# Early transposed chunks and row copies issued from the scalar engine's queue, and the gates and first splits of the second expert product placed ahead of the last chunks

## The chip, the cores and the metric

The kernel runs on one core of one Trainium2 chip. A core has TensorE (PE; its weight loads are shown as PEld), VectorE (DVE), ScalarE (ACT), GpSimd (POOL) and SyncE (SP), each with an instruction queue of its own that runs in order; transfers are issued from the queues of SP, ACT or POOL and carried out by 16 DMA engines. The metric is the device time of one execution in microseconds, the median of several runs; lower is better.

## The reference

One hybrid decoder layer in float32: 256 tokens, model width 1024.

```python
h = rmsnorm(x, mix_norm_g)
rq, rk, rv, rg, mq, mk, mv, ga, gb = split(h @ w_in)            # w_in: 1024 x 6656
ret = retention(rotary(rq), rotary(rk) / 8, rv)                  # 8 heads, chunks of 128, group norm
y_a = (ret * silu(rg)) @ ret_w_branch
att = moba_attention(norm(mq), norm(mk), mv, rel_bias)           # one block of 256: causal softmax with a bias
y_b = att @ moba_w_branch
x = x + (sigmoid(ga) * y_a + sigmoid(gb) * y_b) @ w_out
h2 = rmsnorm(x, ffn_norm_g)
# PEER: 8 heads, 128 x 128 = 16384 experts, the best 16 of each head
q = (h2 @ peer_w_q).reshape(T, 8, 2, 128)
s = einsum('thcd,hcnd->thcn', q, sub_keys)
experts, gates = top16 of the 16 x 16 sums of the two top16, softmax
a = gelu(einsum('td,thkd->thk', h2, u_tab[experts]))
x = x + einsum('thk,thkd->td', gates * a, v_tab[experts])
```

## The kernel before, in words

The order of the instructions on each engine is written by hand: Python loops emit them, and every engine works through its own in that order. There are three stages.

*Mixer and queries* (pieces). Every weight matrix is cut into pieces of 256 rows by 512 columns; `pieces` holds 72 for the mixer (`n_mixer`) and 16 for the PEER queries. In iteration i, `load_to(i + 1)` issues loads into `raw_ring` (six tiles of 512 KB) on SP; `cut(i + 3)` splits a landed piece into a high and a low part (ACT writes `rhi`, L136; DVE writes `rlo`, L137); `products(i)` runs three products of PE for each pair (L217 to L219 or L226 to L228); `pump` advances up to three generators with the epilogues of the units, attention (L348, L354, L366, L367), rotary (L310, L259), retention, and `residual` (L513, L517, transposes L526).

*Early chunks.* The tables `peer_u` and `peer_v` are walked in 128 chunks of 128 experts. The first product of the PEER part needs a chunk of `peer_u` transposed. For one chunk in eight (`STEP`), NPRE = 16 in all, that is done in the mixer stage by `early_turns(i)`: four reads of 128 KB bring a chunk in blocks (L672), two stream transposes on DVE turn it (L677, half a chunk each), and a write stores it in the DRAM tensor `turned` (L674). The buffers `early[0]` (`eraw`, and `h`, the tile `h2`) and `early[1]` (`eT`, and `hTf`) alternate. The reads and writes are issued from SP's queue.

*First expert product* (chunks c = 0 to 127). `transpose_u(c + 2)` turns a chunk by eight transposes of PE into the `turn` banks (L661; four banks, two for each chunk) and two copies of ACT (L662), or, for an early chunk, takes what `load_any` read from `turned`. Then 16 products of PE (L1114) give 144 of the 192 dense tokens their scores; `product_evac` puts a Gelu on them, two chunks at a time (L1075, L1078), POOL multiplies with the gates (L1076). Beside it run

- `gather(GATHER)`, 0.95 steps a chunk: `fetch` gathers rows of `peer_u`, later of `peer_v`, by index on POOL (L911) for the tokens that are not dense; `dot_v` (L922) and the running sum `vacc` (L983 on ACT for the first row, L985 on DVE) take them up;
- `chain_step(BUDGET)`: generators that yield their cost, of which 1.28 are spent a chunk: eight `topk` (t = 0, 1 and q = 0 to 3), then `dense_gates`. This one works on groups of four tokens: `one_hots` builds two sets of one-hots on DVE (L1012, L1013), ACT scales four of them by the gates (L1015), PE multiplies them (L1048) two steps later (`LAG_G`), and `gates_evac` writes the result into `W` (L1059 on DVE, L1061 on ACT). A step costs `GSTEP` = 1.25.

Ahead of the chunks, 24 small copies (L1097) bring rows of `h2x` from DRAM into three tiles `h2r`, issued from SP. At the end of the stage the PSUM pools are closed, `cut_v` splits V chunks (L136, L137), and `cut_w` splits two chunks of the gates `W` into `cw` (L1090 on ACT, L1091 on DVE).

*Second expert product.* For each chunk, eight `block`s of two products (L1140, L1141) accumulate in all eight PSUM banks; `gather(GATHER_V)` takes half a step a chunk. In chunk 125 the copies for the last sums are issued; then DVE adds the gathered sum (L1166, L1167), and `add_up` (L1173, L1174) and `turn_back` (L1179 to L1182) bring the banks back and add them to the residual.

Of the kernel before, what the change touches and what calls it, by code (L numbers as in the profile page):

```python
# [20 lines left out]
P = 128  # L21
# [22 lines left out]
LAG_G = 2  # L44
SCRATCH = 88
TOPK = 16
NPRE = 16
STEP = 128 // NPRE
PRE0 = 4
SK = 16  # L50
NP = H * TOPK
NJ = NP // 2
# [11 lines left out]
def layer_kernel(ctx, tc, x, mix_norm_g, w_in, ret_w_branch, moba_q_gain, moba_k_gain, moba_w_branch,  # L64
# [37 lines left out]
    def lo_tile(dt=F32R):  # L102
        return rg.tile([P, 1024], dt, name="rlo_", tag="rlo", bufs=4)
# [21 lines left out]
    def pump(n=3):  # L125
        for g in list(tasks)[:n]:
            if g in tasks:
                advance(g)
# [494 lines left out]
    def load_any(i):  # L623

        if sk_at <= i < sk_at + 2:
            r = raw_tile().rearrange("p (j i) -> p j i", j=H)
            nc.sync.dma_start(r, peer_sub_keys[0].rearrange("h c n d -> n (h c) d")[:, H * (i - sk_at):H * (i - sk_at + 1), :])
            sk_raw.append(r)
            return
        i -= 2 * (i >= sk_at)  # L630
        if i < len(pieces):
            load(i)
        elif i < len(pieces) + NK:
            c = i - len(pieces)
            if c % STEP == STEP - 1:
                u_raw[c] = raw_tile()
                nc.sync.dma_start(u_raw[c], turned[c // STEP])
            else:
                u_raw[c] = load_rows(peer_u, c)
        elif i < len(pieces) + 2 * NK:  # L640
            v_raw[i - len(pieces) - NK] = load_rows(peer_v, i - len(pieces) - NK)
# [8 lines left out]

    def transpose_u(c):

        if c < NK and c % STEP == STEP - 1:
            u_T[c] = u_raw.pop(c)
        elif c < NK:
            r = u_raw.pop(c)
            u_T[c] = hi_tile(F32)
            for q in range(2):
                p = psum["turn"].tile([P, 512], F32, name="turn")
                for k in range(4):  # L660
                    T.transpose(p[:, k * P:(k + 1) * P], r.rearrange("p (i k) -> p k i", k=KC)[:, 4 * q + k], ident)  # L661
                A.activation(u_T[c][:, 512 * q:512 * (q + 1)], p, AF.Copy)  # L662

    def early_turns(i):

        m, step = divmod(i - PRE0, 4)
        if step == 0 and -1 <= m < NPRE - 1:

            c = STEP * (m + 1) + STEP - 1
            src = peer_u[0, c * P:(c + 1) * P, :].rearrange("(b a) (g d) -> g a b d", a=32, g=4)  # L670
            for g in range(4):
                nc.sync.dma_start(early[0][(m + 1) % 2][32 * g:32 * g + 32].rearrange("a (b d) -> a b d", b=4), src[g])  # L672
        if step == 1 and 0 < m <= NPRE:
            nc.sync.dma_start(turned[m - 1], early[1][(m - 1) % 2])  # L674
        if step % 2 == 0 and 0 <= m < NPRE:
            k = slice(2 * step, 2 * step + 4)
            V.transpose(early[1][m % 2].rearrange("p (k b a) -> p b k a", k=KC, b=4)[:, :, k],  # L677
                        early[0][m % 2].rearrange("p (b i k) -> p b k i", b=4, k=KC)[:, :, k])

# [65 lines left out]
    for i in range(n_mixer + 3):  # L745
        load_to(i + 1)
        cut(i + 3)
        products(i)
        pump()
        early_turns(i)  # L750
    while tasks:
        pump()
    dump("x1", xt)
# [55 lines left out]
    def topk(t, q, s_sb):  # L809
# [60 lines left out]
        if q < 3:  # L870
            return
        g = gates[:, t].rearrange("p (h k) -> p h k", h=H)
        A.activation(g, g, AF.Exp)
        yield 2.0
        sm = tk.tile([P, H], F32, name="sm")
# [131 lines left out]
    def one_hots(oh_buf, t, k, slot):  # L1007

        buf, slot = (oh_buf, slot) if slot < 8 else (oh_more, slot - 8)
        o2, o1 = buf[:, 0, slot:slot + 4], buf[:, 1, slot:slot + 4]  # L1010
        i1, i2 = (tT[:, t, j, k:k + 4, None].to_broadcast([P, 4, NK]) for j in range(2))
        V.tensor_tensor(o2, niota[:, None, :].to_broadcast([P, 4, NK]), i2, op=OP.is_equal)  # L1012
        V.tensor_tensor(o1, iota[:, None, :].to_broadcast([P, 4, NK]), i1, op=OP.is_equal)  # L1013
        for j in range(4):
            A.activation(o1[:, j], o1[:, j], AF.Copy, scale=tT[:, t, 2, k + j:k + j + 1])  # L1015
        return [(o2[:, j], o1[:, j]) for j in range(4)]

    full = []

    def gates_finish():  # L1020
        while full:
            gates_evac(*full.pop())

    def dense_gates():

        def columns(t):
            p = psum["turn"].tile([P, 512], F32, name="turn")
            for j, src in enumerate((i12f[:, t, 0], i12f[:, t, 1], gates[:, t])):
                T.transpose(p[:, j * P:(j + 1) * P], src, ident)
            A.activation(tT[:, t, :3], p[:, :3 * P].rearrange("p (j i) -> p j i", j=3), AF.Copy)  # L1030

        yield 2.0
        columns(1)
        yield 0.1
        V.tensor_scalar(niota, iota, -1.0, None, op0=OP.mult)
        oh_buf = cp.tile([P, 2, 8, NK], F32, name="oh_buf", tag="b8")
        built = []
        for n0 in range(0, ND + 4 * LAG_G, 4):
            gates_finish()
            if n0 == P - 8:  # L1040
                while not gs["xdone"]:
                    gather_step()
                columns(0)
            if len(built) == LAG_G or (n0 >= ND and built):
                n1, oh = built.pop(0)
                p = psum["gates"].tile([P, 512], F32, name="gp")
                for j, (o2, o1) in enumerate(oh):
                    T.matmul(p[:, j * P:(j + 1) * P], o2, o1, start=True, stop=True)  # L1048
                full.append((n1, p.rearrange("p (t i) -> p t i", t=4)))
            if n0 < ND:  # L1050
                t, k0 = (1, n0) if n0 < P else (0, n0 - P + NG)
                built.append((n0, one_hots(oh_buf, t, k0, n0 % 12)))
            yield GSTEP
# [37 lines left out]
            V.tensor_tensor(w[:, :, ND:], W[:, c:c + 2, :], w[:, :, :ND].bitcast(F32), op=OP.subtract)  # L1091
            w_cut[c] = w

    h2r = [lo_tile(F32) for _ in range(NXG)]
    for n in range(NXG):
        for h in range(H):
            nc.sync.dma_start(h2r[n][NXP * h:NXP * (h + 1)], h2x[NXP * n:NXP * (n + 1)])  # L1097
    for c in range(TAHEAD):
        transpose_u(c)
    for c in range(NK):  # L1100
        load_to(len(pieces) + c + TAHEAD)
        gates_finish()
        transpose_u(c + TAHEAD)
        if c and c % 2 == 0:
# [9 lines left out]
            T.matmul(pa[:, n:n + NA], uT[:, k * P:(k + 1) * P], hTf[:, k], start=(c % 2 == 0 and k == 0),  # L1114
                     stop=(k == KC - 1), skip_group_check=True)
        pump()
        gather(GATHER)
        chain_step(BUDGET)
        if c >= NK - 2:
            load_to(len(pieces) + c + 3)  # L1120
            cut_v(c - (NK - 2))
    while chain:
        chain_step(9.0)
        gates_finish()
    product_evac(NK - 2, pa)


    cps.close()
    psum["acc"] = ctx.enter_context(tc.tile_pool(name="psv", bufs=KC, space=bass.MemoryType.PSUM))
    cw = cp.tile([P, 2, D], F32R, name="cw", tag="b8")[:, :, :4 * ND].rearrange("p s (c t) -> p s c t", c=2)  # L1130

    o = [acc() for _ in range(KC)]
    cut_w(0)
    half = P - NG
    res, late = {}, []

# [112 lines left out]
```

## Time and profile before

| | us |
|---|---|
| median of 3 runs | 1028.72 (1023.83 to 1029.67) |
| profiled execution, its time | 1027.87 |
| profiled execution, its span | 1026.1 |
| PE busy in it | 999.1 |
| DVE busy | 812.5 |
| ACT busy | 549.0 |
| POOL busy | 305.3 |

The span runs from the first to the last instruction of the profiled execution; the execution's own time has what lies around it too. Times in the rows of the profile are microseconds from the span's start, unless they are marked as nanoseconds. A line such as L1114 is a line of the kernel before. In a row of waits the engine before the arrow stood idle until the instruction behind it ended. In a row of the timeline the first number is the start and the second the duration; PE's rows are pipelined, so that their durations overlap.

### The profile page before, as it was taken

Reading aid. Unit: us, or ns where it says so; the run is one execution under the profiler, and the core shown is the slowest. Engines: PE = TensorE matmul, PEld = TensorE weight load, DVE = VectorE, ACT = ScalarE, POOL = GpSimd, SP = SyncE. Lnnn points to the kernel's source line nnn. Section 1 sums busy time; section 2 is a strip of 40 time slices with the busy share of each in tenths; the row PEclk is TensorE's granted clock in tenths of the full one; section 3 lists DMA queues with packets and bytes.
Section 4 is the critical chain, followed back from the end, with each engine's and each line's share of the span. In section 5 each row is a group of like instructions: output and inputs, shape, how many; then the busy total and the mean of one; then the engine's idle time right before and its main releaser. Section 6 shows DMA issues by size and latency. Waiting matters only on the chain.

```text
span 1026.1 us, 19479 instructions
## 1 busy us (share of the span) xinstructions
PE 999.1 (97%) x7364; PEld 963.7 (94%) x7364; DVE 812.5 (79%) x1483; ACT 549.0 (54%) x989; POOL 305.3 (30%) x258
## 2 busy tenths in 40 slices
PE   6989999999999999999999999999899999999998
PEld 5877998997998999999999999999899999999997
DVE  5767566879589894699978798973888888888886
ACT  5534554534553435443467687686455555555553
POOL 2411010000103443444343333544433333333310
PEclk9999999999999999999999999999999999999999
DMA  9876665797657997999997767787999999999983
GB/s 319 244 222 195 224 220 172 259 303 240 210 196 245 400 370 283 343 371 383 391 387 264 289 241 263 294 309 280 334 338 346 340 351 336 352 336 355 334 300 111
DMA packets 104123, 301.44 MB, mean 294 GB/s; under 512 B 11052, under 2 KB 21829, under 8 KB 103901
## 3 DMA queue, kind: packets, MB, share of 16 engines
q1 hardware_dynamic: 77164, 204.95, 57.0%
q0 software_dynamic: 26864, 95.25, 25.7%
q8 instruction: 58, 0.95, 0.4%
q14 instruction: 37, 0.30, 0.1%
HBM read 288.62 MB, written 10.95 MB: 292 GB/s over the span
## 4 chain that ended last, share of the span: by engine, by line
PE 87%; DMA 5%; issue 2%; DVE 2%; ACT 2%; POOL 1%; SPq 0%; DVEq 0%; POOLq 0%; ACTq 0%
PE acc L1114 21%; PE acc L1140 20%; PE acc L1141 9%; PE turn L661 8%; PE acc L217 4%; PE acc L226 4%; PE acc L227 3%; PE acc L228 3%; PE acc L218 3%; PE acc L219 3%; PE gp L1048 3%; DMA raw_ring<-in_w_out_dram 2%; PE side L568 1%; POOL rows L911 1%; DMA rows<-in_peer_u_dram,eg 1%
## 5 line engine op out<-in xcount | busy, mean ns | idle before, releaser
L911 POOL DMA_INDIRECT rows<-in_peer_u_dram,eg x112 | 131.8, 1177 | 123.0 <-DVE rows L922 47.2
L911 POOL DMA_INDIRECT rows<-in_peer_v_dram,eg x64 | 103.4, 1616 | 165.4 <-DVE vacc L985 163.8
L661 PE MATMUL turn<-ident,raw_ring 128*128 128x128 f32 x896 | 117.6, 274 | 2.2 <-DMA raw_ring<-in_peer_u_dram 1.3
L661 PEld LDWEIGHTS turn<-ident,raw_ring 128*128 128x128 f32 x896 | 109.0, 191 | 2.8 <-issue 1.8
L922 DVE SCALAR_TENSOR_TENSOR rows<-rows,h 128x1024 f32<-128x1024 f32 x64 | 78.4, 1229 | 18.8 <-DMA rows<-in_peer_u_dram,eg 17.6
L985 DVE SCALAR_TENSOR_TENSOR vacc<-rows,av,vacc 128x1024 f32<-128x1024 f32 x63 | 80.5, 1278 | 14.6 <-ACT vacc L983 12.9
L1090 ACT ACTIVATE cw<-W 128x384 fp32r<-128x384 f32 x64 | 33.7, 527 | 82.6 <-PE acc L1141 36.4
L1091 DVE TENSOR_TENSOR cw<-W,cw 128x384 fp32r<-128x384 f32 x64 | 36.3, 567 | 36.3 <-ACT cw L1090 36.3
L1015 ACT ACTIVATE oh_buf<-oh_buf,tT 128x128 f32<-128x128 f32 x128 | 41.2, 394 | 26.8 <-DVE oh_buf L1013 25.8
L1076 POOL TENSOR_TENSOR W<-W,gl 128x288 f32<-128x288 f32 (+17 forms) x27 | 24.1, 892 | 92.5 <-ACT gl L1075 80.2
L1059 DVE TENSOR_TENSOR W<-gp,W 128x360 f32<-128x360 f32 (+17 forms) x36 | 35.4, 983 | 8.5 <-PE gp L1048 7.2
L1114 PE MATMUL acc<-hTf,raw_ring 128*128 128x144 f32 x256 | 34.0, 286 | 0.0
L1048 PE MATMUL gp<-oh_buf 128*128 128x128 f32 x256 | 33.7, 275 | 0.0
L1114 PEld LDWEIGHTS acc<-hTf,raw_ring 128*128 128x128 f32 x256 | 32.3, 190 | 0.0
L1048 PEld LDWEIGHTS gp<-oh_buf 128*128 128x128 f32 x256 | 31.4, 192 | 0.0
L1061 ACT ACTIVATE W<-gp 128x512 f32<-128x512 f32 (+18 forms) x48 | 28.0, 584 | 6.1 <-DVE W L1059 2.3
L531 POOL DMA_DIRECT2D x1d<-xt x1 | 0.7, 652 | 92.0 <-DVE xt L513 92.0
L922 DVE SCALAR_TENSOR_TENSOR rows<-rows,rlo__3153 128x1024 f32<-128x1024 f32 x16 | 19.4, 1215 | 10.2 <-DMA rows<-in_peer_u_dram,eg 10.2
L143 POOL TENSOR_TENSOR gny<-va,minus_half 128x8 f32<-128x8 f32 x2 | 4.4, 2182 | 76.9 <-DVE va L433 76.9
L1015 ACT ACTIVATE oh_more<-oh_more,tT 128x128 f32<-128x128 f32 x64 | 20.6, 396 | 11.1 <-DVE oh_more L1013 11.1
L1012 DVE TENSOR_TENSOR oh_buf<-niota,tT 128x512 f32<-128x512 f32 x32 | 23.1, 722 | 2.8 <-ACT tT L1030 2.8
L1013 DVE TENSOR_TENSOR oh_buf<-iota,tT 128x512 f32<-128x512 f32 x32 | 22.0, 689 | 0.0
(2082 smaller groups left out, 3476.5 us busy)
## 6 DMA issues: line engine op xcount, KB each, us to landing
raw_ring<-in_peer_v_dram SPq DMA_DIRECT2D x128, 512.0 KB
raw_ring<-in_peer_u_dram SPq DMA_DIRECT2D x112, 512.0 KB
raw_ring<-in_w_in_dram SPq DMA_DIRECT2D x52, 512.0 KB
raw_ring<-in_peer_w_q_dram SPq DMA_DIRECT2D x16, 512.0 KB
raw_ring<-turned SPq DMA_DIRECT2D x16, 512.0 KB
eraw<-in_peer_u_dram SPq DMA_DIRECT2D x32, 128.0 KB
h<-in_peer_u_dram SPq DMA_DIRECT2D x32, 128.0 KB
turned<-eT SPq DMA_DIRECT2D x8, 512.0 KB
```

Source lines behind the costliest of these rows:

```text
L217: T.matmul(o[t], xh[:, s], wh, start=(k == 0), stop=False)
L226: T.matmul(d, wh[:, s], xh, start=(k == 0 and b % 2 == 0), stop=False, skip_group_check=True)
L661: T.transpose(p[:, k * P:(k + 1) * P], r.rearrange("p (i k) -> p k i", k=KC)[:, 4 * q + k], ident)
L911: G.indirect_dma_start(out=r, out_offset=None, in_=tab, in_offset=bass.IndirectOffsetOnAxis(ap=eg[:, j:j + 1], axis=0))
L922: V.scalar_tensor_tensor(r, r, 1.0, h, op0=OP.mult, op1=OP.mult, accum_out=av[:, j:j + 1])
L985: V.scalar_tensor_tensor(gs["acc"], r, av[:, j:j + 1], gs["acc"], op0=OP.mult, op1=OP.add)
L1015: A.activation(o1[:, j], o1[:, j], AF.Copy, scale=tT[:, t, 2, k + j:k + j + 1])
L1048: T.matmul(p[:, j * P:(j + 1) * P], o2, o1, start=True, stop=True)
L1091: V.tensor_tensor(w[:, :, ND:], W[:, c:c + 2, :], w[:, :, :ND].bitcast(F32), op=OP.subtract)
L1114: T.matmul(pa[:, n:n + NA], uT[:, k * P:(k + 1) * P], hTf[:, k], start=(c % 2 == 0 and k == 0), stop=(k == KC - 1), skip_group_check=True)
L1140: T.matmul(o[b][:, :2 * ND], vh[:, n], w, start=(c == 0), stop=False, skip_group_check=True)
L1141: T.matmul(o[b][:, :ND], vl[:, n], w[:, :ND], start=False, stop=(c == NK - 1), skip_group_check=True)
```

## The change

- NPRE is 15, STEP stays 8, and PRE0 is 5: chunk 127 is turned by PE with the others. The reads and the write of an early chunk are issued from ACT's queue, the write at step 3 of the same chunk instead of step 1 of the next; the two transposes stand in neighbouring iterations (steps 0 and 1, not 0 and 2), and `early_turns` runs ahead of `pump`.
- The row copies for `h2r` are issued from ACT's queue, eight in each of the first three chunks.
- In `topk` a `yield 3.0` stands ahead of the Exp. In `dense_gates` the scaling of one-hots on ACT (`factors`) is issued one step after the one-hots, behind PE's products of the step.
- At the end of the first product the gather stops in the last three chunks. In chunk 124 the rest of the chain is issued at once and `cw` is allocated; `cut_v(0)`, `cut_w(0)` and `cut_v(1)` follow in chunks 125, 126 and 127.

```diff
-NPRE = 16
-STEP = 128 // NPRE
-PRE0 = 4
+NPRE = 15
+STEP = 8
+PRE0 = 5
...
-            if c % STEP == STEP - 1:
+            if c % STEP == STEP - 1 and c // STEP < NPRE:
...
             for g in range(4):
-                nc.sync.dma_start(early[0][(m + 1) % 2][32 * g:32 * g + 32].rearrange("a (b d) -> a b d", b=4), src[g])
-        if step == 1 and 0 < m <= NPRE:
-            nc.sync.dma_start(turned[m - 1], early[1][(m - 1) % 2])
-        if step % 2 == 0 and 0 <= m < NPRE:
-            k = slice(2 * step, 2 * step + 4)
+                nc.scalar.dma_start(early[0][(m + 1) % 2][32 * g:32 * g + 32].rearrange("a (b d) -> a b d", b=4), src[g])
+        if step == 3 and 0 <= m < NPRE:
+            nc.scalar.dma_start(turned[m], early[1][m % 2])
+        if step < 2 and 0 <= m < NPRE:
+            k = slice(4 * step, 4 * step + 4)
...
         products(i)
+        early_turns(i)
         pump()
-        early_turns(i)
...
         g = gates[:, t].rearrange("p (h k) -> p h k", h=H)
+        yield 3.0
         A.activation(g, g, AF.Exp)
...
-        for j in range(4):
-            A.activation(o1[:, j], o1[:, j], AF.Copy, scale=tT[:, t, 2, k + j:k + j + 1])
-        return [(o2[:, j], o1[:, j]) for j in range(4)]
+        def factors():
+            for j in range(4):
+                A.activation(o1[:, j], o1[:, j], AF.Copy, scale=tT[:, t, 2, k + j:k + j + 1])
+        return [(o2[:, j], o1[:, j]) for j in range(4)], factors
...
+            if built:
+                built[-1][1][1]()
             if n0 < ND:
...
-    h2r = [lo_tile(F32) for _ in range(NXG)]
-    for n in range(NXG):
-        for h in range(H):
-            nc.sync.dma_start(h2r[n][NXP * h:NXP * (h + 1)], h2x[NXP * n:NXP * (n + 1)])
+    h2r = []
+    def rows_x(n):
+        if n < NXG:
+            h2r.append(lo_tile(F32))
+            for h in range(H):
+                nc.scalar.dma_start(h2r[n][NXP * h:NXP * (h + 1)], h2x[NXP * n:NXP * (n + 1)])
...
         load_to(len(pieces) + c + TAHEAD)
+        rows_x(c)
         gates_finish()
...
-        gather(GATHER)
+        if c < NK - 3:
+            gather(GATHER)
         chain_step(BUDGET)
-        if c >= NK - 2:
+        if c == NK - 4:
+            while chain:
+                chain_step(9.0)
+                gates_finish()
+            cw = cp.tile([P, 2, D], F32R, name="cw", tag="b8")[:, :, :4 * ND].rearrange("p s (c t) -> p s c t", c=2)
+        if c >= NK - 3:
             load_to(len(pieces) + c + 3)
-            cut_v(c - (NK - 2))
-    while chain:
-        chain_step(9.0)
-        gates_finish()
+        if c == NK - 3:
+            cut_v(0)
+        elif c == NK - 2:
+            cut_w(0)
+        elif c == NK - 1:
+            cut_v(1)
     product_evac(NK - 2, pa)
...
-    cw = cp.tile([P, 2, D], F32R, name="cw", tag="b8")[:, :, :4 * ND].rearrange("p s (c t) -> p s c t", c=2)
     o = [acc() for _ in range(KC)]
-    cut_w(0)
```

More of the change, by code (lines that the diff above doesn't have):

```diff
@@ L651, in transpose_u @@
     def transpose_u(c):
-        if c < NK and c % STEP == STEP - 1:
+        if c < NK and c % STEP == STEP - 1 and c // STEP < NPRE:
             u_T[c] = u_raw.pop(c)
@@ L1046, in dense_gates @@
                 p = psum["gates"].tile([P, 512], F32, name="gp")
-                for j, (o2, o1) in enumerate(oh):
+                for j, (o2, o1) in enumerate(oh[0]):
                     T.matmul(p[:, j * P:(j + 1) * P], o2, o1, start=True, stop=True)
                 full.append((n1, p.rearrange("p (t i) -> p t i", t=4)))
+            if built:
+                built[-1][1][1]()
             if n0 < ND:
```

## The prediction

> **What bounds the kernel.** I read the page's busy times first, then the waits of TensorE (PE), then what ended each of them. On the page:
>
> ```profile
> span 1026.1 us, 19479 instructions
> PE 999.1 (97%) x7364; PEld 963.7 (94%) x7364; DVE 812.5 (79%) x1483; ACT 549.0 (54%) x989; POOL 305.3 (30%) x258
> PE 87%; DMA 5%; issue 2%; DVE 2%; ACT 2%; POOL 1%; SPq 0%; DVEq 0%; POOLq 0%; ACTq 0%
> ```
>
> TensorE is busy for 97% of the span and is 87% of the chain that ended last. A change can win only where PE waits (27 us in all), or by leaving PE work out; whatever lies on another engine costs nothing until PE waits for it. The waits of TensorE (us in total, times, longest):
>
> ```profile
> PE acc L1140 <- DVE cw L1091: 4.0, 1, 4.0
> PE side L259 <- POOL ra L310: 1.8, 1, 1.8
> PE side L526 <- DVE xg L517: 1.8, 1, 1.8
> PE gp L1048 <- ACT W L1061: 1.4, 1, 1.4
> PE turn L661 <- DMA raw_ring<-in_peer_u_dram: 1.3, 1, 1.3
> PE side L366 <- ACT pr L354: 1.0, 1, 1.0
> PE acc L218 <- DVE rlo__2252 L137: 0.3, 1, 0.3
> ```
>
> The first is the passage from the first expert product (L1114) to the second (L1140). The windows over it (columns: window, length, busy PE, PEld, DVE, ACT, POOL, granted clock, DMA share, GB/s) show a second loss behind it:
>
> ```profile
> 719.00:723.00 4.00, 0.03 (x1) 0.01 (x1) 3.61 (x4) 3.13 (x5) 3.53 (x4) 1.00 0.76 252
> 724.30:727.80 3.50, 3.50 (x16) 3.50 (x15) 2.88 (x4) 1.06 (x1) 1.69 (x1) 0.51 1.02 417
> ```
>
> PE stands for 4.0 us, and then runs 3.5 us at a granted clock of 0.51: 3.5 x 0.49 = 1.7 us more. The passage costs 5.7 us.
>
> **The change part by part.** *The passage.* Today the splits of the first V chunks and of the gates (`cut_v`, `cut_w(0)`) stand after the last U chunks, and DVE has sums of gathered rows (L985) between them (a product of one chunk from the chain of waits, then the timelines of ACT and DVE):
>
> ```profile
> 606.84 1.96 PE acc L1114 x16
> 715.52 1.05 ACT L136 ACTIVATE rhi__7415<-raw_ring 128x1024 fp32r<-128x1024 f32 x1
> 719.13 0.41 ACT L1075 ACTIVATE gl<-acc 128x288 f32<-128x288 f32 x1 [1.62 <-PE acc L1114]
> 719.44 0.52 ACT L1090 ACTIVATE cw<-W 128x384 fp32r<-128x384 f32 x1
> 719.39 1.28 DVE L985 SCALAR_TENSOR_TENSOR vacc<-rows,av,vacc 128x1024 f32<-128x1024 f32 x1 [0.82 <-DMA rows<-in_peer_v_dram,eg]
> 720.60 1.22 DVE L137 TENSOR_TENSOR rlo__7432<-raw_ring,rhi__7431 128x1024 fp32r<-128x1024 f32 x1
> 721.73 1.15 DVE L1091 TENSOR_TENSOR cw<-W,cw 128x384 fp32r<-128x384 f32 x1
> ```
>
> After the change `cut_v(0)`, `cut_w(0)` and `cut_v(1)` are issued in chunks 125 to 127, with no gather between, while PE still has two to three products of 1.96 us to do. ACT's share in that time is one Gelu (0.41), the gates (0.52) and two splits of 1.05. So only the last Gelu (L1075) stands between the products: 0.4 us. Gain 4.0 + 1.7 - 0.4 = 5.3 (at most 5.7, at least 3 should a PSUM bank or DVE be late).
>
> *The drained gates.* This is the price. Each of the two `topk` tails (t = 0 and 1) gets a `yield 3.0`, together 6.0 of a budget of 1.28 a chunk: the dense gates end 4.7 chunks later. Their last step stands in chunk 121 now; it would be 125 to 126, but all is drained at chunk 124 (NK - 4). Counting the credit step by step, the group products (L1048) popped at n0 = 180 and 184 fall in chunks 122 and 123, and three (188, 192, 196) in chunk 124. In that chunk each group needs its four factors (L1015), which now stand one step ahead of it, behind ACT's other work. From the chain of waits around 690 us and the timelines of PE, ACT:
>
> ```profile
> 608.80 0.89 PE gp L1048 x8
> 609.69 0.89 PE turn L661 x8
> 694.25 0.95 ACT W L1061
> 695.20 0.91 ACT rhi__7205 L662 x2
> 696.11 1.17 ACT oh_more L1015 x4
> 712.11 1.16 ACT L983 ACTIVATE vacc<-rows,av 128x1024 f32<-128x1024 f32 x1
> ```
>
> From the start of chunk 124, ACT (with 0.2 us of latency) takes the last group (0.95), the turned chunk (0.91), a Gelu (0.41), the first gathered V row (1.1), factors (1.17): 4.8; then a group (0.95) and factors (1.17): 6.9. PE's own work before its third group product is 0.89 + 1.96 + 2 x 0.89 = 4.6. PE waits 6.9 - 4.6 = 2.3 us. Without the V row in that place it would be 1.2; with ACT 1.7 late, 4.0. I take 2.3.
>
> *Chunk 127 is turned on PE* (NPRE 15): eight transposes more, the row of 0.89. Cost 0.9, not hidden.
>
> *The last early turn goes away*, and the queue is changed. DVE's timeline just before the residual:
>
> ```profile
> 244.12 1.20 DVE L677 STREAM_TRANSPOSE hTf<-h 128x512 f32<-128x512 f32 x1
> 247.49 1.14 DVE L677 STREAM_TRANSPOSE hTf<-h 128x512 f32<-128x512 f32 x1
> 248.56 1.17 DVE L137 TENSOR_TENSOR rlo__2308<-raw_ring,rhi__2307 128x1024 fp32r<-128x1024 f32 x1
> ```
>
> DVE is late there and PE waits for it: 0.3 (L218) and 1.8 (L526), 2.1 us. The two transposes shown belong to the 16th early chunk and are gone: 2.3 us less on DVE. I book the 2.1 as gained. Below nothing: the other 15 are done in neighbouring pieces and ahead of `pump`, so an epilogue may wait 1.1 us more on DVE; bounds 0 to 2.3.
>
> *Early reads and writes on ACT's queue.* On SP they block what is behind them, the loads of weights (first two rows: the DMA queue's own waits; then durations min/median/max of the issues in ns; the last row is ACT's load in the windows):
>
> ```profile
> SPq L672 <- DVE eT L677: 65.6, 7, 13.5
> SPq L672 <- DVE hTf L677: 49.4, 7, 8.8
> L672 SPq DMA_DIRECT2D eraw<-in_peer_u_dram x32: 328/424/1470, 12.1 to 212.6; - x32
> L1097 SPq DMA_DIRECT2D rlo__3153<-h2x x8: 339/418/419, 309.5 to 312.6; - x8
> 100.00:165.00 65.00, 65.00 (x471) 60.21 (x470) 36.54 (x55) 33.38 (x58) 2.72 (x1) 1.00 0.61 202
> ```
>
> SP waits 115 us for DVE, and still PE is busy for all 65 us of that window: the loads arrive in time but for the places above. No trace of before has a DMA issued by ACT; the nearest row is SP's, 0.42 us, the floor is 0. 15 x 5 issues x 0.42 = 31 us on ACT, 2.1 in every four pieces. Cover: ACT is busy 33.4 of 65, and splits run three pieces ahead of PE (`cut(i + 3)`). The buffers that a read waits for were transposed three pieces earlier, and the write waits two pieces after its transpose, so nothing should be stuck behind it on ACT. Without that cover it would be up to 1.7 us for each burst of four. I take 0 (from -3, if L259 and L366 go too because weights arrive earlier, to +4).
>
> The Trainium skill's page "DMA: Bandwidth & Descriptors", section on issuing engines not being separate DMA queues, says that the engines' DMAs run on the same 16 DMA engines and that spreading them only saves issue time. By that rule alone the move of queue is worth 0.42 us an issue on SP and nothing else; the rows of SP's waits show here another thing that moving frees, the order in one queue, and no run yet shows what it is worth to PE.
>
> *Row copies.* 24 issues (L1097) hold SP ahead of the U loads, after which PE waits 1.3 us (L661 <- DMA). They go to ACT, eight in each of chunks 0, 1 and 2:
>
> ```profile
> 322.98 1.10 ACT L662 ACTIVATE rhi__3193<-turn 128x512 f32<-128x512 f32 x2
> 332.18 1.28 ACT L1078 ACT_TABLE_LOAD   x1
> 333.48 0.41 ACT L1078 ACTIVATE W<-acc 128x288 f32<-128x288 f32 x1
> ```
>
> At 0.42 each a burst is 3.3 us, against a chunk of 1.96 + 0.89 = 2.85 on PE. From the end of the second turned chunk (0): burst, chunk 2 out at 4.3; burst, chunk 3 at 8.6; burst, chunk 4 at 12.9; table and Gelu 1.7. PE has two chunks in four banks ahead; it would wait 0.9 for the bank of chunk 3 and 1.6 for that of chunk 4, 2.5 in all. If half a microsecond of each burst runs beside the activation before it, 1.3; if issuing is free on ACT, 0. I take the middle, 1.3: it eats the 1.3 of the removed wait (net 0, from -1.3 to +1.2).
>
> *Factors one step later.* The 1.4 of L1048 <- ACT stems from ACT waiting for DVE's one-hots in a chunk with two steps (chunk 91; it would be 83). ACT no longer waits for a fresh one-hot; I book 1.2 gained (0 to 1.4). The Exp placed later waits less on DVE, which PE does not see: 0.
>
> *The tail.* Three chunks without gather: four V rows fetched before the second product instead of seven, so at one step in two chunks the last sum moves from chunk 118 to 124. There DVE has no room:
>
> ```profile
> 1010.80 1.23 DVE L137 TENSOR_TENSOR rlo__10378<-raw_ring,rhi__10377 128x1024 fp32r<-128x1024 f32 x1 [0.39 <-ACT rhi__10377 L136]
> 1013.19 1.22 DVE L1167 TENSOR_TENSOR raw_ring<-raw_ring,rows 64x1024 f32<-64x1024 f32 x1
> 1014.77 0.35 DVE L1174 TENSOR_TENSOR turned<-turned,acc 128x192 f32<-128x192 f32 x1 [0.36 <-ACT turned L1173]
> ```
>
> A sum (1.28) ahead of the last split, with 0.4 idle before it, delays L1174 by 0.9. Cost 0.9 (0 to 2, since the copy of its upper half then lands late too).
>
> *Sum:* -5.3 + 2.3 + 0.9 - 2.1 + 0 + 0 - 1.2 + 0.9 = -4.5. The profiled execution took 1027.87, so 1023.4; the median of the three runs, 1028.72, lies 0.85 above it, and they spread from 1023.83 to 1029.67. I forecast 1023.2, with 0.2 for a wait on late weights here and there.
>
> **The rivals.** *B, the SP queue was worth more:* the 115 us of SP's waits delay weights all through the mixer, and without them ACT and DVE have their work earlier, so that L259 and L366 (2.8 us) vanish as well, and ACT's issues hide (another 1.3). 1023.2 - 4.1 = 1019.1. Against it, from the waits of all engines:
>
> ```profile
> DVE pr L348 <- DMA bias<-skew: 7.8, 1, 7.8
> ```
>
> Both waits follow this slow load of the attention's biases, which stays.
>
> *C, the move of queue gives nothing:* PE's waits at the residual come from the residual's own splits on DVE, and stay (+2.1), as does part of the wait on one-hots (+0.6). 1025.9, within 0.5% of before. The page's rule on issuing engines would end here.
>
> *D, slower: ACT becomes the bound of the mixer.* A burst of four reads holds ACT 1.7 us, and what PE waits for in the same piece (a PSUM evacuation by L260 or L367) stands behind it. At 0.7 us of each of 15 bursts the change loses its gain (10 us), at all 1.7 it is 25: some 1034 to 1038. Against it: ACT's busy half of the window.
>
> **How the numbers follow.** My own case has 0.45, with 1020 to 1026 for itself; B 0.20; C 0.24; D 0.11. Half a per cent, 5.1 us, is about what a measurement of this kernel tells from no change: the line is at 1023.6. Of my own case 0.28 lies below it, with B 0.48 faster; the other 0.17 with C 0.41 the same; D 0.11 slower. For 8 in 10 the range takes in B and C with the bounds of the drained gates and of the copies, 1017 to 1028.5.
>
> **What would show it.** Right: no PE wait at L1140, granted clock 1.00 behind it; a new wait of 1 to 4 us at L1048 in chunk 124, on ACT L1015; no SPq wait at L672; L526 below 0.5; eight more L661 for chunk 127; L1174 first at a microsecond later against the last L1140. The DMA issues on ACT's own timeline give the price that I bounded. Wrong: PE waits at L662's consumers in chunks 3 to 6 above 2.5 us, new waits in the mixer on ACT, or a longer drain.

## The result, and the profile after

| | us | ratio to the kernel before |
|---|---|---|
| before, median of 4 runs | 1029.07 (1023.83 to 1029.67) | 1 |
| after, median of 4 runs | 1041.70 (1038.96 to 1043.42) | 1.0132, 95% interval 1.0090 to 1.0174 |
| after, profiled execution | 1043.05, span 1041.3 | |

The changed kernel is slower by 13.6 us by that ratio (12.6 by the medians), where 1023.2 was forecast. Two lines of its page stand against those of before:

```profile
span 1041.3 us, 19486 instructions
PE 1008.7 (97%) x7372; PEld 972.8 (93%) x7372; DVE 814.4 (78%) x1481; ACT 546.1 (52%) x991; POOL 305.1 (29%) x255
```

The shares say nothing new: PE is 97% busy as before, and ACT is a little less busy than it was. What changed is in PE's waits (us in total, times, longest):

```profile
PE side L703 <- DVE hn L700: 7.6, 1, 7.6
PE turn L661 <- ACT rhi__3258 L662: 5.5, 1, 5.5
PE turn L661 <- ACT rhi__3183 L662: 4.5, 1, 4.5
PE turn L661 <- ACT rhi__3223 L662: 3.4, 1, 3.4
PE side L259 <- POOL ra L310: 1.8, 1, 1.8
PE acc L1198 <- DVE turned L1193: 1.5, 2, 1.2
...
PE gp L1052 <- ACT oh_more L1018: 0.6, 1, 0.6
PE acc L1159 <- ACT gl L1081: 0.6, 1, 0.6
```

The first row is PE's wait at the very start of the kernel. It is the longest of before too (7.5 us there, though the prediction's list of waits leaves it out), and no part of the change touches it. The wait at the passage between the products (L1140 before, L1159 now) fell from 4.0 to 0.6 us, the waits at L526 and for fresh U loads are gone, and three new waits have come: 13.4 us of PE waiting for ACT to empty a `turn` bank, in the first chunks. The windows over that stretch, of the kernel after (columns: window, length, busy PE, PEld, DVE, ACT, POOL, granted clock, DMA share, GB/s):

```profile
320.00:360.00 40.00, 25.62 (x156) 24.32 (x155) 34.59 (x109) 10.06 (x19) 15.18 (x14) 0.79 0.97 291
352.00:358.00 6.00, 5.15 (x24) 4.75 (x25) 5.96 (x10) 5.00 (x9) 4.42 (x3) 0.57 0.76 238
739.10:743.00 3.90, 3.90 (x27) 3.90 (x28) 3.03 (x4) 3.26 (x4) 2.79 (x2) 1.00 0.71 175
```

and of the kernel before, the first row from the stretch in which it issued the copies on SP:

```profile
309.00:317.00 8.00, 8.00 (x69) 8.00 (x68) 7.83 (x58) 0.00 (x0) 2.53 (x3) 1.00 0.48 135
320.00:360.00 40.00, 37.90 (x318) 37.52 (x318) 35.10 (x109) 19.11 (x37) 17.17 (x15) 1.00 1.03 373
```

PE executes 156 of its products in these 40 us where it executed 318. At 37.90/318 = 0.119 us each, the missing 162 are 19.3 us. The spans differ by 15.2, so the rest of the change gained about 4 us. The loss has two parts, the waits (13.4), and the granted clock behind them (0.57 in 352 to 358 and 0.79 over the 40 us, where it was 1.00). The third row is the start of the second product, now at clock 1.00: there the change did what it was forecast to do.

ACT's own waits in that stretch, kernel after:

```profile
ACT rhi__3258 L662 <- DMA rlo__3249<-h2x: 10.2, 1, 10.2
ACT rhi__3183 L662 <- DMA rlo__3174<-h2x: 8.7, 1, 8.7
ACT rhi__3223 L662 <- DMA rlo__3214<-h2x: 7.0, 1, 7.0
```

These activations (L662) read nothing that the row copies write; they only stand behind the copies (L1107) on ACT's queue. ACT's timeline of the kernel after shows the queue (rows marked ACTq are issues of transfers: start, us from the first start to the last end, how many):

```profile
323.53 8.98 ACTq L1107 DMA_DIRECT2D rlo__3174<-h2x  x7
332.62 1.09 ACT L662 ACTIVATE rhi__3183<-turn 128x512 f32<-128x512 f32 x2 [8.71 <-DMA rlo__3174<-h2x]
333.87 6.74 ACTq L1107 DMA_DIRECT2D rlo__3214<-h2x  x8
340.71 0.60 ACT L662 ACTIVATE rhi__3223<-turn 128x512 f32<-128x512 f32 x1 [7.01 <-DMA rlo__3214<-h2x]
...
348.09 3.50 ACTq L1107 DMA_DIRECT2D rlo__3249<-h2x  x7
351.96 1.08 ACT L662 ACTIVATE rhi__3258<-turn 128x512 f32<-128x512 f32 x2 [10.17 <-DMA rlo__3249<-h2x]
```

Eight issues of 0.42 us were forecast as 3.3 us; the three bursts took ACT 8.7, 7.0 and 10.2. Yet an issue itself is not dear. The rows of lines L1107 and L672 (duration in ns min/median/max) have the price that was bounded in advance:

```profile
L672 ACTq DMA_DIRECT2D eraw<-in_peer_u_dram x32: 317/443/1117, 18.0 to 219.3; - x32
L1107 ACTq DMA_DIRECT2D rlo__3214<-h2x x8: 308/309/434, 333.9 to 340.3; - x8
```

The time lies between the issues. Each issue in the trace's records names the semaphore that its transfer will raise when it lands, and the one that it waits for. Some issues of the kernel after (time of the issue, engine, what is moved, semaphore, the transfer that used it last, and when that one's last completion arrived):

```
 327.42 ACT rlo__3174<-h2x  103   SP  raw_ring<-in_peer_u_dram, issued 322.23   landed 327.403
 329.77 ACT rlo__3174<-h2x  104   ACT rlo__3174<-h2x,           issued 323.14   landed 329.751
 331.49 ACT rlo__3174<-h2x  107   SP  raw_ring<-turned,         issued 323.13   landed 331.464
 333.87 ACT rlo__3214<-h2x  109   SP  raw_ring<-in_peer_u_dram, issued 324.03   landed 333.845
 338.12 ACT rlo__3214<-h2x  107   ACT rlo__3174<-h2x,           issued 331.49   landed 338.096
 348.09 ACT rlo__3249<-h2x  101   SP  raw_ring<-in_peer_u_dram, issued 338.37   landed 348.065
```

Each of these started about 0.02 us after the landing of the transfer before it on the same semaphore. The transfers of SP and ACT take turns on eight such semaphores (100 to 104, 107 to 109), and an issue whose turn comes to one still in flight waits, with everything behind it on its engine. Ten of the 24 copies started in this way on a landing, four on SP's loads and six on ACT's own copies. A view of the profile has the same thing from the other side, the DMA queue's own waits in the kernel after, 318 to 360 us:

```profile
SPq L616 <- PE turn L661: 18.0, 5, 12.5
SPq L616 <- DMA raw_ring<-in_peer_u_dram: 11.1, 1, 11.1
SPq L616 <- DMA rlo__3249<-h2x: 9.9, 1, 9.9
SPq L616 <- DMA rlo__3214<-h2x: 3.0, 1, 3.0
```

In the first row the load waits for a tile of its ring that PE still reads. In the third and fourth a load of `peer_u` on SP waits for the row copies on ACT, with which it has no data in common.

### The profile page after: what moved, and what is told of

It reads as the page before. It is cut to its first block, busy times and chain, and to the rows that moved or that the text cites. A ratio compares the mean times of both kernels' runs of the same rounds, so it can differ in the third digit from the quotient of the medians.

```text
span 1041.3 us, 19486 instructions
## 1 busy us (share of the span) xinstructions
PE 1008.7 (97%) x7372; PEld 972.8 (93%) x7372; DVE 814.4 (78%) x1481; ACT 546.1 (52%) x991; POOL 305.1 (29%) x255
## 4 chain that ended last, share of the span: by engine, by line
PE 91%; DMA 5%; DVE 1%; ACT 1%; issue 1%; POOL 0%; SPq 0%; ACTq 0%; DVEq 0%; POOLq 0%
PE acc L1126 24%; PE acc L1159 19%; PE turn L661 9%; PE acc L1160 8%; PE acc L226 4%; PE acc L227 4%; PE acc L228 4%; PE gp L1052 4%; PE acc L217 3%; PE acc L218 3%; PE acc L219 3%; DMA raw_ring<-in_peer_u_dram 2%; DMA raw_ring<-in_w_in_dram 2%; PE side L568 1%; PE side L371 1%
## 5 line engine op out<-in xcount | busy, mean ns | idle before, releaser
L912 POOL DMA_INDIRECT rows<-in_peer_u_dram,eg x112 | 138.8, 1240 | 128.2 <-DVE rows L923 49.0
L661 PE MATMUL turn<-ident,raw_ring 128*128 128x128 f32 x904 | 121.2, 278 | 14.1 <-ACT rhi__3258 L662 5.5
L661 PEld LDWEIGHTS turn<-ident,raw_ring 128*128 128x128 f32 x904 | 111.8, 192 | 15.0 <-ACT rhi__3258 L662 5.8
L923 DVE SCALAR_TENSOR_TENSOR rows<-rows,h 128x1024 f32<-128x1024 f32 x64 | 77.7, 1217 | 7.7 <-DMA rows<-in_peer_u_dram,eg 7.7
L1065 DVE TENSOR_TENSOR W<-gp,W 128x328 f32<-128x328 f32 (+17 forms) x36 | 36.6, 1017 | 7.3 <-PE gp L1052 7.0
L1082 POOL TENSOR_TENSOR W<-W,gl 128x288 f32<-128x288 f32 (+17 forms) x24 | 16.1, 669 | 86.0 <-ACT gl L1081 79.8
L923 DVE SCALAR_TENSOR_TENSOR rows<-rows,rlo__3174 128x1024 f32<-128x1024 f32 x16 | 19.3, 1214 | 20.3 <-DMA rows<-in_peer_u_dram,eg 20.3
L1052 PE MATMUL gp<-oh_buf 128*128 128x128 f32 x256 | 33.8, 276 | 0.0
L1126 PE MATMUL acc<-hTf,raw_ring 128*128 128x144 f32 x240 | 31.9, 286 | 0.0
L1052 PEld LDWEIGHTS gp<-oh_buf 128*128 128x128 f32 x256 | 31.5, 191 | 0.1
L923 DVE SCALAR_TENSOR_TENSOR rows<-rows,rlo__3249 128x1024 f32<-128x1024 f32 x16 | 19.4, 1219 | 9.7 <-DMA rows<-in_peer_u_dram,eg 9.7
L1014 DVE TENSOR_TENSOR oh_buf<-iota,tT 128x512 f32<-128x512 f32 x32 | 25.6, 799 | 0.0
```

The lines of the kernel that those rows point to most:

```text
L912: G.indirect_dma_start(out=r, out_offset=None, in_=tab, in_offset=bass.IndirectOffsetOnAxis(ap=eg[:, j:j + 1], axis=0))
L923: V.scalar_tensor_tensor(r, r, 1.0, h, op0=OP.mult, op1=OP.mult, accum_out=av[:, j:j + 1])
```

## The experiments

**Theory W.** The loss is the row copies on ACT alone: each waits at its issue for a landing, ACT's copies L662 stand behind it, and PE behind those. **Rivals:** that ACT's part in the early chunks costs in the mixer (the prediction's D); that the end of the first product costs (the drained gates); that issuing on ACT, or the copies' bytes, are dear in themselves.

### Which part of the change

The kernel after with the copies back on SP:

```diff
-    def rows_x(n): ...   nc.scalar.dma_start(h2r[n]...)     # in chunks 0 to 2
+    for n in range(NXG): ...   nc.sync.dma_start(h2r[n]...) # ahead of the chunks
```

> The changed kernel with the 24 row copies back on SP's queue ahead of the chunks, all else as changed. Theory 1 (the loss is the row copies standing in ACT's queue, each waiting for a completion semaphore that an earlier transfer holds): the three waits of PE on L662 (4.5, 3.4 and 5.5 us) and the half clock behind them go, about 18 us, and the wait of 1.3 us for a U load comes back: 1024 us, faster than before by 0.5%. Theory 2 (the loss is spread, issues on ACT slow the whole first half): less than half comes back, 1034 us.

Measured: 1024.41 (12 runs), ratio 0.9966 (0.9945 to 0.9988), so it is faster than before. Its PE waits have none at L662, and the window holds 326 products:

```profile
320.00:360.00 40.00, 38.77 (x326) 38.39 (x325) 35.11 (x110) 19.56 (x37) 17.72 (x15) 1.00 1.03 376
```

The kernel before with nothing but the copies moved:

```diff
-    nc.sync.dma_start(h2r[n]...)     # ahead of the chunks
+    nc.scalar.dma_start(h2r[n]...)   # eight in each of chunks 0 to 2
```

> The kernel before with only the row copies moved to ACT's queue, eight in each of chunks 0 to 2. Theory 1: PE waits on L662 in chunks 2 to 4 and the clock falls, 14 to 18 us slower than before: 1045 us. Theory 2, a price of 0.42 us an issue: 1.3 to 2.5 us slower at most, 1031 us.

Measured: 1047.56 (4 runs), ratio 1.0177 (1.0143 to 1.0211): 18.2 us slower (14.7 to 21.7). PE's waits are the three of the kernel after:

```profile
PE turn L661 <- ACT rhi__3265 L662: 5.7, 1, 5.7
PE turn L661 <- ACT rhi__3230 L662: 4.1, 1, 4.1
PE turn L661 <- ACT rhi__3190 L662: 3.9, 1, 3.9
```

The kernel before with the early chunks as changed (NPRE 15, reads and writes on ACT, order), the rest as it was:

```diff
-NPRE = 16
+NPRE = 15
-                nc.sync.dma_start(early[0]...)
+                nc.scalar.dma_start(early[0]...)
```

> The kernel before with only the early turns changed: 15 of them, reads and writes on ACT's queue, transposes in neighbouring pieces ahead of the pump. Theory 1: gains 2.4 us ahead of the residual, costs 0.9 us for chunk 127 and about 2.3 us of half clock after the attention's wait at 66 to 72 us: 1030 us, the same as before. Theory 2: 1035 us or more.

Measured: 1027.46 (12 runs), ratio 0.9991 (0.9969 to 1.0013), no difference that can be told. ACT waits in the mixer for landings, in this kernel:

```profile
ACT rhi__1269 L136 <- DMA eraw<-in_peer_u_dram: 3.0, 1, 3.0
ACT ret L440 <- DMA eraw<-in_peer_u_dram: 2.4, 1, 2.4
```

Here are waits of the same kind as in the chunks, up to 3.0 us each, and PE has no new wait in the mixer for them. That the splits run three pieces ahead would explain it; no run varied it. Rival D had the mechanism, an ACT held by its issues, but the wrong place for it.

The kernel before with the changes at the two products alone (credit of 3.0, factors a step later, gather stopped, drain, first splits):

```diff
+        yield 3.0
         A.activation(g, g, AF.Exp)
...
-        gather(GATHER)
+        if c < NK - 3:
+            gather(GATHER)
```

> The kernel before with only the parts of the two products changed: yield ahead of the Exp, factors a step later, no gather in the last three chunks, the chain drained at chunk 124, first splits ahead of the last chunks; early turns and row copies as before. Both theories: the passage gains 5, the factors 1.5, the drain costs 0.8, the tail 0.9: 1024 us, 0.5% faster.

Measured: 1025.05 (12 runs), ratio 0.9956 (0.9940 to 0.9972): 4.5 us faster (2.9 to 6.2). The three parts add up: copies +18.2, early chunks -0.9, end -4.5 make +12.8, and the whole change was measured at +13.6.

### What in the copies costs

Three edits spread them in time or change their number. First two in each of chunks 0 to 11, on ACT:

```diff
-    eight copies in each of chunks 0, 1, 2
+    for j in range(2 * c, 2 * c + 2): ...   # two in each of chunks 0 to 11
```

> The changed kernel with the same 24 row copies on ACT's queue, two in each of chunks 0 to 11 instead of eight in each of 0 to 2. Theory 1 (each transfer takes over one of eight completion semaphores, and its issue waits until the transfer eight places earlier in the program has landed): with two copies and one load a chunk that one was issued nearly three chunks ago and has landed; ACT waits little, 1024 us like the version with the copies on SP. Theory 2 (ACT pays a high price for every issue, whatever is in flight): 24 issues cost what they cost, 1036 to 1042 us. Theory 3 (the copies' bytes hold up the U loads): the same bytes in four times the time, between the two.

Measured: 1031.41 (10 runs), ratio 1.0026 (1.0002 to 1.0051). Against the version with the copies on SP (0.9966) 6 of 17 us remain, and the part of the expectation that a transfer eight turns back would have landed was wrong: in a crowded stretch the U loads were in flight for 8 to 14 us (one issued at 326.94 landed at 335.37, one of 353.10 after 366). PE has two waits at L661 on ACT L662, 3.0 and 2.5 us. By its time alone the run is what Theory 3 forecast, between the two others; but its PE waits end with ACT, and none with a U load.

Then bursts of eight, eight chunks apart:

```diff
-        rows_x(c)
+        if c % 8 == 0:
+            rows_x(c // 8)
```

> The changed kernel with the bursts of eight copies on ACT set apart, in chunks 0, 8 and 16. Theory 1: each burst of eight still goes once round the eight semaphores and meets the U loads that are in flight, so each still costs some 4 us of PE and the half clock: 1036 to 1042 us, little less than the changed kernel. If the bursts only met each other (the copies of the burst before): the second and third cost nothing, 1030 us.

Measured: 1034.62 (10 runs), ratio 1.0063 (1.0039 to 1.0088), below the 1036 to 1042 of Theory 1 and above the 1030 of bursts that only meet each other. Three waits of PE at L661 remain, 3.4, 3.3 and 2.0 us, each alone. Against the version with the copies on SP, 10 of 17 us remain: some 7 came from the bursts following one another, and a burst by itself still costs.

Then the same 24 copies at the same places of the program, from POOL's queue:

```diff
-                nc.scalar.dma_start(h2r[n]...)
+                nc.gpsimd.dma_start(h2r[n]...)
```

> The changed kernel with the 24 row copies on POOL's queue, eight in each of chunks 0 to 2: the same bytes at the same time, but nothing of them stands in ACT's queue. Theory 1: PE does not wait on L662, 1024 to 1027 us; gathers start some 4 us a chunk later on POOL. Theory 3 (bytes): PE waits as in the changed kernel, 1040 us.

Measured: 1026.71 (10 runs), ratio 0.9988 (0.9965 to 1.0011). PE's waits at L662 are gone. But POOL comes to these places earlier than ACT, as the issues show (the burst between them starts at 313.0):

```profile
L1107 POOL DMA_DIRECT2D rlo__3174<-h2x x8: 484/484/510, 309.1 to 312.5; - x8
L1107 POOL DMA_DIRECT2D rlo__3249<-h2x x8: 489/529/565, 318.6 to 323.0; - x8
```

The last of the 24 went out when the changed kernel issued its first (323.1), so the time of the copies was not kept, against the expectation, and this run does not rule out that their bytes, moved at the crowded time, make the loss. The copies with fewer bytes, below, bear on that. A new wait stands in this kernel, from 538 us on:

```profile
PE turn L1033 <- DVE gates L879: 4.3, 1, 4.3
```

DVE computes these gates behind dot products (L923) that waited four times for gathered rows, 1.2 to 2.0 us each.

Then three copies of 512 KB, each reading its rows eight times, on ACT:

```diff
-            for h in range(H):
-                nc.scalar.dma_start(h2r[n][NXP * h:NXP * (h + 1)], h2x[NXP * n:NXP * (n + 1)])
+            nc.scalar.dma_start(h2r[n], <the rows of h2x, repeated by a leading dimension of 8 with step 0>)
```

> The changed kernel with three copies on ACT instead of 24, one in each of chunks 0 to 2, each bringing 16 rows eight times over: the same bytes into the same tiles. Theory 1: one transfer a chunk, whose semaphore was last held eight transfers ago, by one that has landed: 1023 us, the best so far. Theory 2: a price for an issue, an eighth of it: 1025 us. Theory 3 (bytes): 1040 us.

Measured: 1031.73 (10 runs), ratio 1.0027 (1.0002 to 1.0053). It misses all three forecasts (1023, 1025, 1040). ACT no longer waits at its issues (0.58 to 1.17 us each), and PE no longer waits for L662; instead SP's loads of `peer_u` wait 8.1 and 5.6 us for the landing of a copy. PE's waits in this kernel:

```profile
PE turn L1033 <- DVE gates L879: 5.7, 1, 5.7
PE turn L661 <- DMA raw_ring<-in_peer_u_dram: 4.7, 4, 2.0
```

U loads wait for the semaphore of a copy, as W says, now for long ones: by the records these three landed 15, 24 and 32 us after their issue. That accounts for the second row; the first, the longer, is the wait for DVE's gates that the run before has too, and how the copies bring it about was not followed up.

### The wait itself

The kernel after with its copies on ACT untouched, and the U loads of chunks 0 to 19 issued by POOL, whose transfers use other semaphores:

```diff
-                nc.sync.dma_start(u_raw[c], ...)
+                (nc.gpsimd if c < 20 else nc.sync).dma_start(u_raw[c], ...)
```

> The changed kernel, its 24 row copies on ACT's queue as they are; only the U loads of chunks 0 to 19 are issued by POOL instead of SP. Theory 1 (a copy on ACT waits at its issue until the transfer that last used its completion semaphore has landed; SP and ACT share eight of them, POOL's queue has others): ACT's copies can then wait only for ACT's own copies, which land about 6.6 us after their issue. The first burst goes out without a wait; the two others wait up to 3 us each instead of 7.0 and 10.2. PE's three waits at L661 on ACT L662 (5.5, 4.5, 3.4) fall to 5 us or less in sum, and the time to 1029 to 1035. Theory 2 (issuing on ACT is itself dear, or the copies are slow because of the bytes they carry beside the loads): bytes, queue and issues of the copies are the same, so the waits stay, and the time is 1039 to 1044. Either way POOL's loads may come late behind gathers in POOL's order, which would show as PE waits at L661 on DMA and not on ACT.

Measured: 1039.01 (6 runs), ratio 1.0089 (1.0057 to 1.0121). ACT's timeline of this kernel (line numbers are three higher):

```profile
321.23 4.34 ACTq L1110 DMA_DIRECT2D rlo__3174<-h2x  x7
325.67 0.60 ACT L665 ACTIVATE rhi__3183<-turn 128x512 f32<-128x512 f32 x1 [4.05 <-issue]
...
326.18 6.47 ACTq L1110 DMA_DIRECT2D rlo__3214<-h2x  x7
332.76 0.60 ACT L665 ACTIVATE rhi__3223<-turn 128x512 f32<-128x512 f32 x1 [6.01 <-DMA rlo__3174<-h2x]
```

and PE's waits:

```profile
PE turn L1036 <- DVE gates L882: 4.0, 1, 4.0
PE turn L664 <- ACT rhi__3223 L665: 3.9, 1, 3.9
PE turn L664 <- ACT rhi__3258 L665: 2.9, 1, 2.9
```

The first burst waits for nothing, as W has it; the second (and the third, 6.5 us) waits for ACT's own copies of the burst before, and 13 of these 16 issues start on such a landing, each eight turns back. PE's waits at the banks are half of what they were, 6.8 against 13.4 (5 or less was expected). The time, 1039.0, is above the range of Theory 1 and at the lower end of Theory 2's (1039 to 1044), so it is the waits and not the time that speak for W. The part that the theory did not have is the wait of 4.0 for DVE's gates, with a clock of half behind it:

```profile
551.80:558.60 6.80, 5.09 (x22) 5.09 (x23) 6.18 (x14) 2.38 (x7) 3.19 (x3) 0.50 0.72 227
```

These two are worth some 7 us as an estimate (4.0, and up to half of 6.8), and without them the time would lie in the range of Theory 1. The first burst of this kernel gives the bare price: eight issues without a wait hold ACT for 4.05 us, so that about 12 of the 25.9 us that ACT lost in the changed kernel are issues, and 14 are waits.

Next, the copies with one sixteenth of their bytes. This kernel leaves out 960 of the 1024 columns, so that its result is not that of the layer; only its times are of use:

```diff
-                nc.scalar.dma_start(h2r[n][NXP * h:NXP * (h + 1)], h2x[NXP * n:NXP * (n + 1)])
+                nc.scalar.dma_start(h2r[n][NXP * h:NXP * (h + 1), :64], h2x[NXP * n:NXP * (n + 1), :64])
```

> The changed kernel with its 24 row copies on ACT, each of 64 columns instead of 1024 (the rest of the three tiles is set to zero by POOL before the chunks, so the second gather's dots are over 64 columns only). Theory 1 (waits for shared completion semaphores): the copies land sooner, so the waits for ACT's own copies of eight places back go, but those for SP's U loads (landing 6.3 us after their issue) stay: PE's waits at L661 on ACT L662 keep a third to two thirds of their 13.4 us, time 1030 to 1037. Theory 2 (the copies' bytes, 0.5 MB a burst, are what delays everything): one sixteenth of the bytes, so the waits nearly vanish, below 2 us, time 1024 to 1027. Theory 3 (the issue itself, 0.44 us each, 10.6 us in all on ACT): nothing changes, waits above 11 us, time 1039 to 1044.

Measured: 1033.16 (10 runs), ratio 1.0038 (1.0017 to 1.0060). ACT's waits, 318 to 360 us:

```profile
ACT rhi__3227 L662 <- DMA rlo__3147<-h2x: 7.8, 1, 7.8
ACT rhi__3261 L662 <- DMA rlo__3148<-h2x: 4.9, 1, 4.9
ACT rhi__3188 L662 <- DMA rlo__3146<-h2x: 4.6, 1, 4.6
```

17.3 us instead of 25.9, with 4 KB a copy instead of 64. PE's longest wait in that stretch:

```profile
340.40 1.97 PE L661 MATMUL turn<-ident,raw_ring 128*128 128x128 f32 x8 [5.70 <-issue]
```

The view puts it down to no engine, but it ends 0.05 us after the first activation of ACT behind the second burst (339.75 and 0.60). With 1.3 us at L661 on ACT's rhi__3261 PE waits 7.0 us for ACT, half of 13.4, as Theory 1 had it; Theory 2 had less than 2, Theory 3 more than 11, and the time lies in the range of Theory 1. So bytes are a part of the loss and not the whole: the bare issues (some 3 x 4.05 of ACT's time) and a wait for a U load (3.2 us, in the second burst) stay.

Last, where the copies stand on ACT. The changed kernel with 16 of them issued by ACT before the last query product, where ACT was idle for 9.2 us, and eight on SP:

```diff
+        if i == len(pieces) - 1:          # ahead of products(i), the last piece
+            h2r = [lo_tile(F32) for _ in range(2)]
+            ...   nc.scalar.dma_start(h2r[n]...)
```

> The changed kernel; of the 24 row copies 16 are issued by ACT ahead of its work for the last query product, where the trace shows ACT idle for 9.2 us (308 to 317 us) and the kernel before had the DMA engines busy for 0.48 of the time; the last eight go back to SP. In chunks 0 to 2 ACT issues none. Theory 1 (the wait at an issue is as long as the transfer before it on its completion semaphore takes to land, and it costs only what waits behind it on ACT): in the quiet stretch a copy lands in about 2 us and nothing on ACT is due, so PE has no wait at L661 on ACT L662 and the time is 1023 to 1027, that of the same kernel with all copies on SP (1024.4, ratio 0.9966). Theory 2 (copies on ACT's queue cost by themselves, wherever they stand): two thirds of the 17 us stay, 1033 to 1038. A third outcome, if the second burst of eight is late for want of a free tile and delays the query product's evacuation at L559: up to 3 us, 1026 to 1029.

Measured: 1023.46 (5 runs), ratio 0.9939 (0.9912 to 0.9967). ACT's timeline in it:

```profile
306.95 3.64 ACTq L996 DMA_DIRECT2D rlo__3077<-h2x  x8
310.70 6.68 ACTq L996 DMA_DIRECT2D rlo__3078<-h2x  x8
317.48 1.08 ACT L559 ACTIVATE W<-acc 128x512 f32<-128x512 f32 x2 [11.78 <-DMA rlo__3078<-h2x]
```

ACT stands idle for 11.8 us ahead of L559, of which 9.2 were idle in the kernel after too, and PE sees a wait of 2.6 us at L568 (the third outcome, without its loss of time) and none at L661 on L662. The second burst did not go out freely: by the records the last of its issues waited until 317.05 for an own copy issued at 312.04, and it cost no time that can be told. ACT's queue is not dear by itself; it is dear in front of work that PE waits for. What no run did is to issue the copies from SP or POOL at the crowded time, 323 to 351 us.

### A better version

The kernel with all copies on SP, and without the credit of 3.0 ahead of the Exp:

```diff
-        yield 3.0
         A.activation(g, g, AF.Exp)
```

> The version that the runs so far point to: the changed kernel with the 24 row copies on SP ahead of the chunks (1024.4 in its own run, ratio 0.9966), and in addition without the two credits of 3.0 before the gates' Exp, so that the dense gates end some 4.7 chunks earlier and less is left to drain at chunk 124. If the drain still costs the 0.8 us that the changed kernel's trace shows at L1052 and in the factors' wait, 1023.6, ratio about 0.996; if the credits protected something (the Exp waiting on ACT for DVE's sums ahead of a turned chunk's evacuation), 1025 to 1028 with a new PE wait at L661 on ACT L662 in the chunks before 100.

Measured: 1024.01 (8 runs), ratio 0.9942 (0.9920 to 0.9964). This and the version with 16 copies in ACT's idle stretch are the fastest; both beat the kernel before and the changed one, and the runs do not tell them from each other or from the one with copies on SP alone (0.9945 to 0.9988). So the credit is not shown to cost or to protect anything.

## Why the prediction was wrong, by its steps

- **Row copies: the step that failed.** Booked at net 0 (-1.3 to +1.2); measured at +18.2 alone (14.7 to 21.7), and 17.1 as the difference between the changed kernel and the one with copies on SP (1.0132 and 0.9966 of 1029). The issue's price was nearly right (0.42 taken; 0.31 to 0.44 at the median). The working took the sum of eight prices for the time of a burst, 3.3 us, found 2.5 us of waits for PE by it, and booked 1.3 of them. Even without any wait a burst holds ACT for 4.05; with waits it was 7.0 to 10.2, PE waited 13.4, and then ran on a lower clock, where the prediction had carried the clock's loss for the passage (1.7) but not for this stall.

What the trace of before had of it: the duration of an issue comes from SP's row, in a stretch where no one waited behind it; the spaces between issues were not looked at. The DMA queue's own waits of the kernel before hold the sign:

```profile
SPq L1097 <- DMA rlo__3154<-h2x: 1.7, 2, 1.2
...
SPq L616 <- DMA rlo__3155<-h2x: 1.1, 2, 0.6
```

A copy waits there for the copies of the tile before it, which it does not read. Most of the 24 went out in a quiet place: 309 to 317 us, with the DMA share of 0.48 in the row shown above; the first landed some 2 us after its issue (309.47 to 311.56). So the change moved the copies twice, to another queue and into another stretch. In chunks 0 to 2 the share is about 1, U loads stand between the copies, and a copy takes 5.7 to 7.0 us at the median of its burst.

- **The passage:** -5.3; PE's wait went from 4.0 to 0.6, and the clock behind it from 0.51 to 1.00 (1.7): -5.1. Right.
- **The drained gates:** +2.3; the wait at L1052 is 0.6, below the lower of the two values worked out (1.2). The V row stood where the working put it (L984, at 726.89). But the third group's product did not wait for all of its four factors, as the working has it; it began at 730.36, when the first had ended (730.30 by the records):

```profile
729.92 1.25 ACT L1018 ACTIVATE oh_more<-oh_more,tT 128x128 f32<-128x128 f32 x4
730.36 1.35 PE L1052 MATMUL gp<-oh_more 128*128 128x128 f32 x8 [0.60 <-ACT oh_more L1018]
```

- **Chunk 127 on PE** and **the last early turn:** +0.9 and -2.1, in sum -1.2; measured together with the move to ACT's queue -0.9 (-3.2 to +1.3). The wait at L526 is gone, and eight more transposes stand in PE's count (7372 against 7364).
- **Early reads and writes on ACT:** 0; held. The buffers were free as argued, but ACT waited for landings all the same (5.4 us in two waits of the changed kernel), and PE has no wait for it.
- **Factors:** -1.2; the wait of 1.4 at L1048 is gone. **The tail:** +0.9; PE's wait for DVE's L1174 (L1193 now) went from 0.6 us to 1.5. Both right. The passage, drain, factors and tail together were forecast at -3.3 and measured at -4.5 (-6.2 to -2.9).
- **The sum.** -4.5 from 1027.87 is 1023.4, and 0.2 more for late weights is 1023.6; the forecast of 1023.2 took the 0.2 off. From the median, 1028.72, it would be 1024.2. With the copies left on SP the rest of the change gained 3.5 us (1.2 to 5.7, by the ratio of 0.9966), so that the sum without this one term held.
- **The rivals.** D forecast 1034 to 1038 with 0.11 and is the nearest in time, by another stretch than its own; none had ACT as the bound in the first chunks. The sign named in advance as proof of a wrong forecast, PE waits behind L662 above 2.5 us in chunks 3 to 6, is what came.
- **The rule on issuing engines** (the Trainium skill, "DMA: Bandwidth & Descriptors", section on issuing engines not being separate DMA queues: DMAs run on the same 16 DMA engines whoever issues them, and issuing from several engines saves issue time alone) would have made the move worth little in either direction. The measurements differ: the same 24 copies cost 18 us on ACT in the chunks, and nothing that can be told on SP or POOL (from 309 or 310 to 323 us), or (16 of them) in ACT's idle stretch.

## What to carry to other kernels

Where transfers share completion semaphores, as here, a transfer that is moved to another engine's queue can cost that engine not only its issue but the wait for whatever used its semaphore last, and this may be another engine's load. So price a move by the landing times of the stretch it moves into, look in the DMA queue's own waits for transfers that wait for transfers they share no data with, and ask what stands behind the issue: put it where nothing that the bound engine needs is next. Ask of every stall of TensorE in a forecast whether the granted clock falls behind it: it did behind those of the changed kernel (0.79 over 40 us), and not behind one of 3.4 us in the run with the bursts set apart (1.00 from 382.5 to 389.5 us).

## What the runs showed of the hardware

- A copy of 64 KB lands in about 2 us where the DMA share is 0.48, and in 5.7 to 7.0 where it is near 1; a load of 512 KB took up to 14 us in such a stretch of the run with two copies a chunk, and 6.3 at the median of the changed kernel's U loads.
- The three copies with a leading repeat of eight landed 15, 24 and 32 us after their issue, and behind a first one at the issue the records hold 7, 8 and 8 completions for them, where a copy of 16 rows or a load has up to 16 (some records are missing). That fits the Trainium skill, "DMA: Bandwidth & Descriptors", section "Rules for kernel authors": an outermost dimension below 16, such as a leading repeat, confines a transfer to as many DMA engines.
